# A two-layer decoder: where a projection group's last transpositions stand, and low parts in halves

## The chip, the cores and the metric

One core of a Trainium2 chip runs the whole program. The metric is the device time of one execution in microseconds (us), the median of several runs.

## The reference, cut to what matters

The program is a trunk of two layers over 2048 positions of width 1024, in float32. Layer A projects the normalised input to queries, keys, values, a forget logit per head and a gate, and attends causally with 16 heads. Layer B projects shared keys and values (4 heads), queries (16 heads) and a gate, and attends in a window of 128. Each attention ends with a gated output projection and a residual.

```python
u = rmsnorm(h, norm_a_g[i])
proj = u @ w_in_a[i]                       # q | k | v | forget logits | gate
q = rmsnorm(q.reshape(b, s, N_HEADS_A, HEAD_DIM), qnorm_a_g[i])
k = rmsnorm(k.reshape(b, s, N_HEADS_A, HEAD_DIM), knorm_a_g[i])
...
k_s, v_s = jnp.split(u_kv @ w_kv, [KV_WIDTH_B], axis=-1)
...
q, gate = jnp.split(u @ w_in_b[j], [WIDTH_B], axis=-1)
q = partial_rope(rmsnorm(q.reshape(b, s, N_Q_HEADS_B, HEAD_DIM), qnorm_b_g[j]), positions)
o = swa_sink_attention(q, k_shared, v_shared, sinks[j])
h = h + (o * jax.nn.silu(gate)) @ w_out_b[j]
```

## The kernel before, in words

Every float32 product is made of three products of rounded parts: a number is split into a high part (ACT rounds it, one copy) and a low part (DVE subtracts), and high x high, high x low and low x high are summed in PSUM.

`projections` runs twice, once for each layer. Its outer loop goes over column groups of the input weights: in layer A values, two key groups, three query groups (the first with the forget logits) and values again; in layer B the shared keys and values, two query groups and two gate groups. For a group, `weights` loads and splits its 8 weight tiles (ACT line 486, DVE line 487; `wh` and `wl` have nine buffers each, so the next group's tiles come in as the last block lets go of the old ones; the raw columns come through `wr`, two buffers of two tiles). Then, but for gate groups, comes a loop over the 16 blocks of 128 positions: 24 products of up to 512 columns (line 759) into one of three `b2` buffers of PSUM, and the block's norm (`qk_norm`: square on ACT, sums, reciprocal root and product on DVE; in layer B the rotary step too, partly on POOL, ending at DVE line 512), which leaves `qn` (two buffers).

`qn` must be transposed. That is `finish`: two to four transpositions on PE (line 349) into `pa` for even blocks and `pb` for odd ones, an eviction by ACT (line 524) and by DVE (line 525) into a staging tile `st`, and after each second block four stores on the SP queue (line 532). `finish` is not called at once but queued in the list `late`; with `QK_LAG = 1`, block t's job is taken out after the products of block t+2. So two jobs, those of blocks 14 and 15, are left when a group ends, and the loop `for job in late` calls them there, before the next group's weights and products.

`jobs` are side tasks of layer A at blocks 0, 3, 6 and 9 of each later group: splitting the gate's weight through three `st` tiles, or spilling the split input. A gate group (line 722) has 16 tiles of 24 products, into `pb` and `b2` (later `pa`) in turn, each followed by a gate evaluation on DVE, ACT and DVE. During the last gate group attention of layer B begins, through a hook.

`attention_b` is a generator of steps. In steps 4 to 11 `weight_split` makes the output weight's parts: a raw tile of two times 512 columns comes through `wr` (line 1420), ACT makes the high part (line 1433), DVE the low part (line 1434), each over 1024 columns. The output projection's products (line 1453) use them later. The exponentials of a step run on ACT at line 1323, the low parts of the transposed attention weights on DVE at line 1349.

The source order is not the order on an engine. A planner places the instructions at build time by its own estimate of durations: of those it takes to be ready, the one that stands first in the source. On the chip each engine then follows that order.

Of the kernel before, what the change touches and what calls it, by code (L numbers as in the profile page):

```python
# [18 lines left out]
ALU = mybir.AluOpType  # L19
# [41 lines left out]
QK_LAG = 1  # L61
# [37 lines left out]
def f_(ap):  # L99
    return ap.bitcast(F32)  # L100
# [51 lines left out]
class Trunk:  # L152
# [471 lines left out]
    def projections(self, normed, groups, row, later=None, pre=None, hook=None, first=None):  # L624

        nc, tc = self.nc, self.tc
        norm, factor, uh, ul, factors, _ = normed
        raw0 = None
        if pre is not None:
            raw0 = self.sb("big", [P, NDT, CH])

            def load_raw(dt):
                g0 = groups[0]
                nc.sync.dma_start(  # L640
                    out=raw0[:, dt : dt + 2, :],
                    in_=g0["w"][dt * P : (dt + 2) * P, g0["c0"] : g0["c0"] + CH].rearrange(
                        "(k p) c -> p k c", p=P
                    ),
                )

            norm(
                1,
                [partial(self.load_vectors, self.loads[:1])]
                + [partial(load_raw, dt) for dt in range(0, NDT, 2)],  # L650
            )
        else:
            norm(1)
        SW = 2 * P
        stages = {}
        z, forget = None, []

        def finish(q, qn, tb):
            t0 = (tb * P) % SW
            np_ = q["nh"] // 2  # L660
            if t0 == 0:
                stages[0] = tuple(self.sb("st", [P, np_, SW]) for _ in range(2))
            self.qk_transpose(qn, q["nh"], q["gain"], stages[0], t0, ("pa", "pb")[tb % 2])
            if t0 + P == SW:
                self.qk_store(
                    stages[0], q["dst"], q["p0"], np_, tb * P - t0, SW, q["hi_first"]
                )

        jobs = []
        if later is not None:  # L670
            wg, cg, gain, spill, wsplit = later

            def spill_u(ch, k, c0):
                t = (uh, ul)[k]
                c = slice(c0, c0 + NDT // 2)
                tc.keep_in_program_order(
                    nc.sync.dma_start(
                        out=spill[ch, k, c].rearrange("c p t -> p c t"), in_=f_(t[ch][:, c])
                    )
                )  # L680

            def split_w(dt):
                g = gain[:, dt : dt + 1]
                raw, hi, lo = (self.sb("st", [P, D]) for _ in range(3))
                nc.sync.dma_start(out=raw, in_=wg[dt * P : (dt + 1) * P, cg : cg + D])
                nc.scalar.activation(r_(hi), raw, AF.Copy, scale=g)
                nc.vector.scalar_tensor_tensor(r_(lo), raw, g, hi, ALU.mult, ALU.subtract)
                for k, t in enumerate((hi, lo)):
                    nc.sync.dma_start(
                        out=wsplit[:, :, dt // 2, k, dt % 2, :].rearrange("f p x -> p f x"),  # L690
                        in_=t.rearrange("p (f x) -> p f x", x=P),
                    )

            jobs = [partial(split_w, dt) for dt in range(NDT)]
            jobs += [
                partial(spill_u, ch, k, c0)
                for ch in range(NCH) for k in range(2) for c0 in (0, NDT // 2)
            ]

        for gi, grp in enumerate(groups):  # L700
            x2 = grp.get("extra")
            n = grp["n"] + (x2[1] if x2 else 0)
            if gi or first is None:
                W = self.weights(
                    grp["w"], grp["c0"], grp["n"], grp["gain"], x2, ahead=None if gi else raw0
                )
            else:
                W = first
            if gi == 0:
                norm(2)  # L710
            if "gate" in grp:
                f0, dst = grp["gate"]
                for ch in range(NCH):
                    rows = self.factor_rows(row, ch)
                    for ft in range(CH // P):
                        if hook is not None and gi == len(groups) - 1:
                            hook(ch * (CH // P) + ft)

                        ps = self.ps(("pb", "pa" if "fl" in self.banks else "b2")[ft % 2], [P, CH])
                        for dt in range(NDT):  # L720
                            for i, (k, u) in enumerate(((0, uh), (0, ul), (1, uh))):
                                nc.tensor.matmul(  # L722
                                    ps, W[k][dt][:, ft * P : (ft + 1) * P], u[ch][:, dt, :],
                                    start=(dt == 0 and i == 0),
                                    stop=(dt == NDT - 1 and i == 2),
                                )

                        sg = self.sb("sq", [P, CH])
                        nc.vector.tensor_tensor(sg, ps, rows, ALU.mult)
                        nc.scalar.activation(ps, sg, AF.Tanh)  # L730
                        nc.vector.scalar_tensor_tensor(sg, ps, 1.0, sg, ALU.add, ALU.mult)
                        fr = f0 + ft * P
                        nc.sync.dma_start(
                            out=dst[fr : fr + P, ch * CH : (ch + 1) * CH], in_=sg
                        )
                continue
            q, v = grp.get("qk"), grp.get("v")
            rope = self.rotary(q["rope"]) if q and "rope" in q else None
            late = []
            for tb in range(NTB):  # L740
                norm(tb + NORM_AHEAD)
                if gi == 1 and tb == ROW_AT:
                    self.rstd_row(factors, row)
                r0 = factors[:, tb : tb + 1]
                if gi == 0 and pre is not None and tb in pre:
                    pre[tb]()
                if tb in FORGET_AT and forget:
                    forget.pop(0)()
                if gi and tb in JOBS_AT and jobs:
                    jobs.pop(0)()  # L750
                us = slice(tb % 4 * P, (tb % 4 + 1) * P)
                ps = self.ps("b2", [P, CH])
                for dt in range(NDT):
                    if hook is not None and gi == len(groups) - 1:
                        hook(tb, dt)
                    if gi == 0:
                        factor(tb, dt)
                    for i, (u, k) in enumerate(((uh, 0), (uh, 1), (ul, 0))):
                        nc.tensor.matmul(  # L759
                            ps[:, :n], u[tb // 4][:, dt, us], W[k][dt],  # L760
                            start=(dt == 0 and i == 0), stop=(dt == NDT - 1 and i == 2),
                        )
                if len(late) > QK_LAG:
                    late.pop(0)()
                if q is not None:
                    c0 = q["c0"]
                    qn = self.qk_norm(
                        ps[:, c0 : c0 + q["nh"] * HD], q["nh"], tb, rope, r0
                    )
                    late.append(partial(finish, q, qn, tb))  # L770
                if grp.get("forget"):
                    if z is None:
                        z = self.sb("rot", [P, NTB, H])
                    nc.vector.scalar_tensor_tensor(
                        z[:, tb, :], ps[:, n - H : n], r0, self.bf, ALU.mult, ALU.add
                    )
                if v is not None:
                    self.v_tile(
                        ps[:, v["c0"] : v["c0"] + v["nh"] * HD], v["nh"],
                        v["dst"][v["h0"] : v["h0"] + v["nh"], tb * P : (tb + 1) * P, :].rearrange(  # L780
                            "h t e -> t h e"
                        ),
                        r0,
                    )
            for job in late:
                job()
            if grp.get("forget"):
                forget = self.forget(z)
        for job in forget:
            job()  # L790
# [467 lines left out]
    def attention_b(self, w_out, res, dst):  # L1258
# [168 lines left out]
        def weight_split(j):  # L1427
# [3 lines left out]
            h, lo = (W[half][t // 4][:, k, t % 4 : t % 4 + 2, :] for k in range(2))  # L1431
            raw = raws.pop(j)
            nc.scalar.copy(h, raw)
            nc.vector.tensor_tensor(lo, raw, f_(h), ALU.subtract)

        load(0)
        load_v(0)
# [185 lines left out]
```

## Time and profile before

| | us |
|---|---|
| median of 3 runs | 2460.58 |
| lowest, highest | 2459.92, 2462.29 |
| the profiled execution | 2461.66 |
| its span (first to last instruction) | 2459.7 |
| mean granted TensorE clock | 0.999 of full speed |

The profile is of one execution. A row of a timeline gives an instruction or several alike in a row; "idle before, and what ended it" is inferred from the semaphores. Products are pipelined, so their durations overlap: the step from start to start is the time that a product takes from PE. PE stands for TensorE's products and transpositions, PEld for its weight loads, DVE for VectorE, ACT for ScalarE, POOL for GpSimd, SP for the queue that issues the DMAs.

### The profile page before, as it was taken

The numbers are of one execution on the slowest core, as the hardware profiler recorded it, in microseconds if no ns is written. First come the engines' busy times: TensorE is split into PE (matmuls) and PEld (weight loads), VectorE is DVE, ScalarE is ACT, GpSimd is POOL, SyncE is SP. The second block draws the span as 40 slices with busy tenths as digits, with TensorE's granted clock in tenths as the row PEclk, the third lists the DMA queues.
The fourth block names the chain that finished last, engine by engine and source line by source line (L and its number), as shares of the span: only waits on it lengthen the run. The fifth ranks groups of instructions, "written<-read, shape, count | busy, mean of one in ns | idle before, by whom it ended". The sixth has DMA issues, their size and how long they took to land.

```text
span 2459.7 us, 36240 instructions
## 1 busy us (share of the span) xinstructions
PE 2424.1 (99%) x12016; PEld 2022.4 (82%) x12016; DVE 1727.4 (70%) x3826; ACT 1255.1 (51%) x2504; POOL 1001.9 (41%) x643
## 2 busy tenths in 40 slices
PE   8999999999999999999999999999999999999999
PEld 6788899988888887878877778888788888888887
DVE  7656567735888888888888866456766523777776
ACT  5433324323777777777777761135323312555554
POOL 0000000012877777777778862210011000377775
PEclk9999999999999999999999999999999999999999
DMA  6656545687554655465456649975434415555552
GB/s 181 207 165 193 156 145 168 192 261 223 168 155 128 210 141 150 143 198 164 133 168 182 169 137 306 290 253 153 139 90 120 137 64 165 174 176 178 180 180 73
DMA packets 351515, 419.24 MB, mean 170 GB/s; under 512 B 64928, under 2 KB 248256, under 8 KB 345152
## 3 DMA queue, kind: packets, MB, share of 16 engines
q1 hardware_dynamic: 351328, 416.92, 56.6%
q8 instruction: 95, 1.56, 0.3%
q14 instruction: 92, 0.75, 0.1%
HBM read 265.29 MB, written 151.40 MB: 169 GB/s over the span
## 4 chain that ended last, share of the span: by engine, by line
PE 46%; DVE 4%; DMA 2%; ACT 2%; POOL 2%; issue 2%; SPq 0%; DVEq 0%; ACTq 0%; POOLq 0%
PE b L759 9%; PE b L1240 5%; PE pa L1027 5%; PE pb L1453 4%; PE pb L722 3%; PE pb L1066 3%; PE b L722 3%; PE mx L936 2%; PE sc L985 2%; PE sc L984 2%; PE pa L1383 1%; PE b L1304 1%; PE pa L722 1%; PE pa L1240 1%; PE pb L1240 1%
## 5 line engine op out<-in xcount | busy, mean ns | idle before, releaser
L759 PE MATMUL b<-wh,big 128*128 128x512 f32 (+3 forms) x2560 | 770.1, 375 | 9.8 <-ACT wh L486 8.7
L1003 POOL TENSOR_TENSOR big<-st,big 128x1024 fp32r<-128x1024 f32 (+1 forms) x320 | 657.9, 2070 | 261.4 <-ACT big L1002 155.6
L759 PEld LDWEIGHTS b<-wh,big 128*128 128x128 f32 x2560 | 471.3, 188 | 81.2 <-ACT wh L486 10.5
L759 PE MATMUL b<-wl,big 128*128 128x512 f32 (+3 forms) x1280 | 474.2, 371 | 1.9 <-DVE wl L487 1.9
L1012 DVE TENSOR_TENSOR ac<-ac,st 128x512 f32<-128x512 f32 (+3 forms) x576 | 355.4, 617 | 55.6 <-ACT st L999 27.2
L999 ACT ACTIVATE st<-sc 128x512 f32<-128x512 f32 (+1 forms) x512 | 274.3, 585 | 161.8 <-PE sc L985 79.0
L1027 PE MATMUL pa<-big 128*128 128x512 f32 (+3 forms) x1280 | 326.1, 369 | 3.9 <-POOL big L1003 1.8
L1002 ACT CAST big<-st 128x1024 fp32r<-128x1024 f32 (+1 forms) x320 | 295.6, 924 | 7.8
L759 PEld LDWEIGHTS b<-wl,big 128*128 128x128 f32 x1280 | 241.4, 189 | 38.3 <-DVE wl L487 6.1
L1027 PEld LDWEIGHTS pa<-big 128*128 128x128 f32 x1280 | 222.0, 189 | 50.3 <-ACT sq L1035 17.0
L947 DVE CUSTOM_DVE_ANT_0 mx<-mx,rot 128x128 f32<-128x128 f32 (+3 forms) x240 | 210.7, 878 | 40.9 <-PE mx L936 34.8
L495 ACT ACTIVATE sq<-b,r 128x512 f32<-128x512 f32 (+2 forms) x128 | 77.8, 608 | 301.6 <-PE b L759 298.6
L984 PE MATMUL sc<-big 128*128 128x512 f32 (+3 forms) x640 | 230.1, 364 | 1.3 <-DVE st L542 1.1
L985 PE MATMUL sc<-big 67*128 67x512 f32 (+3 forms) x640 | 229.0, 367 | 0.0
L936 PE MATMUL mx<-big 66*128 66x128 f32 (+3 forms) x660 | 191.1, 363 | 3.6 <-DVE mt L947 3.1
L1066 PE MATMUL pb<-wh,wr 128*128 128x512 f32 x488 | 179.3, 398 | 2.8 <-DMA wr<-wg 2.2
L859 POOL MEMSET rot<- 128x1024 bf16 x1 | 1.0, 952 | 420.8 <-PE pb L349 420.8
L497 DVE TENSOR_REDUCE sm<-sq 128x8 f32<-128x512 f32 (+2 forms) x128 | 74.9, 585 | 138.6 <-ACT sq L495 138.4
L1352 POOL TENSOR_TENSOR big<-big,tri 128x1024 fp32r<-128x1024 f32 x60 | 143.8, 2397 | 67.1 <-DVE big L1349 62.2
L936 PEld LDWEIGHTS mx<-big 66*128 66x128 f32 x660 | 114.1, 190 | 40.9 <-DVE mt L947 11.9
L984 PEld LDWEIGHTS sc<-big 128*128 128x128 f32 x640 | 121.0, 189 | 23.1 <-DVE st L542 1.5
L985 PEld LDWEIGHTS sc<-big 67*128 67x128 f32 x640 | 121.2, 189 | 21.0
(281 smaller groups left out, 4124.8 us busy)
## 6 DMA issues: line engine op xcount, KB each, us to landing
wr<-wg SPq DMA_DIRECT2D x62, 512.0 KB
va<-st SPq DMA_DIRECT2D x32, 512.0 KB
ka<-st SPq DMA_DIRECT2D x64, 256.0 KB
ut<-big SPq DMA_DIRECT2D x16, 1024.0 KB
big<-ka SPq DMA_DIRECT2D x16, 1024.0 KB
big<-qa SPq DMA_DIRECT2D x16, 1024.0 KB
qb<-st SPq DMA_DIRECT2D x64, 256.0 KB
big<-qb SPq DMA_DIRECT2D x16, 1024.0 KB
```

Of the source, the lines that this page charges most:

```text
L722: nc.tensor.matmul(ps, W[k][dt][:, ft * P : (ft + 1) * P], u[ch][:, dt, :], start=(dt == 0 and i == 0), stop=(dt == NDT - 1 and i == 2),)
L759: nc.tensor.matmul(ps[:, :n], u[tb // 4][:, dt, us], W[k][dt], start=(dt == 0 and i == 0), stop=(dt == NDT - 1 and i == 2),)
L936: mm = nc.tensor.matmul(ps[:, b, :wb], qb[:66, i * P : (i + 1) * P], kb[:66, k0 + b * wb : k0 + (b + 1) * wb], start=True, stop=True,)
L947: nc.vector.tensor_tensor_reduce(out=lg, in0=lg, in1=mask, scale=1.0, scalar=NEG, op0=ALU.add, op1=ALU.max, accum_out=f_(o),)
L984: nc.tensor.matmul(o, ka[:, ks], qa[:, qs], start=not (last and n_), stop=False)
L985: nc.tensor.matmul(o, kb[:, ks], qb[:, qs], start=False, stop=not diag)
L999: nc.scalar.activation(pf[:, off : off + w], ps[:, :w], AF.Exp, scale=HD**-0.5)
L1002: nc.scalar.copy(ph[:, :tw], pf[:, :tw])
L1003: nc.gpsimd.tensor_tensor(pl[:, :tw], pf[:, :tw], f_(ph[:, :tw]), ALU.subtract)
L1012: nc.vector.tensor_tensor(a_, a_, pf[:, off : off + w], ALU.add)
L1027: nc.tensor.matmul(pv[:, q0 : q0 + w], v[:, k, :], src[:, off : off + w], start=(p == 0 and n_ == 0 and i == 0), stop=(last and n_ == 1 an ...
L1066: nc.tensor.matmul(ps, w[:, dt // 2 % 2, wk, dt % 2, :], us[dt][uk], start=(dt == 0 and i == 0), stop=(dt == NDT - 1 and i == 2),)
```

## The change

`late` is made once, ahead of the loop over the groups, and is no longer emptied at the end of each: the jobs of blocks 14 and 15 are taken out in the next group, after its products of blocks 0 and 1 (in a gate group after the products of its first two tiles; in the group of values, which queues none of its own, one after each block until the list is empty). Only after the last group whatever is left would be called. In `attention_b` the low part of the output weight is made by two DVE operations of 512 columns in place of one of 1024.

```diff
@@ projections
         stages = {}
+
+        late = []
         z, forget = None, []
...
                                     stop=(dt == NDT - 1 and i == 2),
                                 )
+                        if late:
+                            late.pop(0)()
 
                         sg = self.sb("sq", [P, CH])
...
             rope = self.rotary(q["rope"]) if q and "rope" in q else None
-            late = []
             for tb in range(NTB):
...
-                if len(late) > QK_LAG:
+                if late and (len(late) > QK_LAG or q is None):
                     late.pop(0)()
...
-            for job in late:
-                job()
+            if gi == len(groups) - 1:
+                for job in late:
+                    job()
@@ attention_b, weight_split
             nc.scalar.copy(h, raw)
-            nc.vector.tensor_tensor(lo, raw, f_(h), ALU.subtract)
+
+            for k in range(2):
+                nc.vector.tensor_tensor(lo[:, k], raw[:, k], f_(h)[:, k], ALU.subtract)
```

## Rows read from the trace of the kernel before

**Rows 1.** The page's first part: each engine's busy time in us, its share of the span, and its count of instructions.

```profile
PE 2424.1 (99%) x12016; PEld 2022.4 (82%) x12016; DVE 1727.4 (70%) x3826; ACT 1255.1 (51%) x2504; POOL 1001.9 (41%) x643
```

**Rows 2.** The list of who waited for whom, PE alone: PE's tile and line, what it waited for, us in total, times, the longest.

```profile
PE b L759 <- ACT wh L486: 8.7, 3, 8.2
...
PE pa L349 <- DVE qn L512: 1.0, 2, 0.5
...
PE pb L349 <- DVE qn L512: 0.6, 1, 0.6
```

**Rows 3.** PE's timeline at the end of layer B's first query group: start and duration in us, line, operation, out<-in, shapes, count, and in brackets the idle time before it with what ended it. `pa` takes the transpositions of even blocks, `pb` those of odd ones. The last row is from the chain that ended last: 24 products of 512 columns in a gate group.

```profile
1842.52 0.60 PE L349 MATMUL pa<-ident,qn 128*128 128x128 f32 x4
...
1842.87 0.48 PE L759 MATMUL b<-wh,big 128*128 128x512 f32 x1
...
1848.46 0.60 PE L349 MATMUL pb<-ident,qn 128*128 128x128 f32 x4
...
1849.57 0.63 PE L349 MATMUL pa<-ident,qn 128*128 128x128 f32 x4 [0.52 <-DVE qn L512]
...
1856.44 0.39 PE L759 MATMUL b<-wl,big 128*128 128x512 f32 x1
...
1856.88 0.63 PE L349 MATMUL pb<-ident,qn 128*128 128x128 f32 x4
...
1990.72 5.44 PE pb L722 x24
```

**Rows 4.** PE's timeline again: the first four rows where the key/value group hands over to the first query group, the last four where the second query group hands over to the first gate group.

```profile
1753.04 0.38 PE L349 MATMUL pb<-ident,qn 128*128 128x128 f32 x2
...
1753.43 0.41 PE L349 MATMUL pa<-ident,qn 128*128 128x128 f32 x2
...
1758.94 0.61 PE L759 MATMUL b<-wh,big 128*128 128x512 f32 x2
...
1760.20 0.41 PE L349 MATMUL pb<-ident,qn 128*128 128x128 f32 x2 [0.65 <-DVE qn L512]
...
1944.26 0.60 PE L349 MATMUL pb<-ident,qn 128*128 128x128 f32 x4
...
1945.38 0.63 PE L349 MATMUL pa<-ident,qn 128*128 128x128 f32 x4 [0.53 <-DVE qn L512]
...
1951.99 0.61 PE L722 MATMUL b<-big,wh 128*128 128x512 f32 x2
...
1952.70 0.63 PE L349 MATMUL pb<-ident,qn 128*128 128x128 f32 x4
```

**Rows 5.** The timeline in layer A: PE at the end of the first key group (two rows; the third is SP, the DMA queue, with the key stores of one pair of blocks), then PE at the first products of the fifth group and of the last.

```profile
199.43 0.60 PE L349 MATMUL pb<-ident,qn 128*128 128x128 f32 x4
...
199.86 0.60 PE L349 MATMUL pa<-ident,qn 128*128 128x128 f32 x4
...
200.98 3.18 SPq L532 DMA_DIRECT2D ka<-st  x4
...
374.43 0.44 PE L759 MATMUL b<-wh,big 128*128 128x384 f32 x1 [0.20 <-ACT wh L486]
...
503.59 0.50 PE L759 MATMUL b<-wl,big 128*128 128x512 f32 x1 [0.29 <-DVE wl L487]
```

**Rows 6.** The timeline of DVE at the end of layer B's first query group (three rows) and of ACT where layer A's last group begins (two rows).

```profile
1849.13 0.29 DVE L512 TENSOR_TENSOR qn<-ro,ro 128x128 f32<-128x128 f32 x1 [0.49 <-POOL ro L511]
...
1851.01 0.75 DVE L525 SCALAR_TENSOR_TENSOR st<-pa,g_qb,st 128x512 fp32r<-128x512 f32 x1 [0.15 <-ACT st L524]
...
1851.83 0.70 DVE L487 SCALAR_TENSOR_TENSOR wl<-wr,g_b,wh 128x512 fp32r<-128x512 f32 x1
...
498.86 0.72 ACT L486 ACTIVATE wh<-wr,g_a 128x512 fp32r<-128x512 f32 x1 [1.17 <-DMA wr<-in_w_in_a]
...
502.03 1.34 ACT L486 ACTIVATE wh<-wr,g_a 128x512 fp32r<-128x512 f32 x2 [1.11 <-DMA wr<-in_w_in_a]
```

**Rows 7.** Prices. First two rows of the view of line 1434 (count, then min/median/max in ns, first and last start; then who waited for it, us and times), then two groups of instructions with each shape apart (busy us, mean ns of one, idle before).

```profile
L1434 DVE TENSOR_TENSOR big<-wr,big x8: 1194/1216/1648, 2105.4 to 2156.0; 128x1024 fp32r<-128x1024 f32 x8
...
  PEld pb L1453: 0.5, 1
...
L1349 DVE TENSOR_TENSOR big<-fl,big 128x512 fp32r<-128x512 f32 x64 | 43.6, 682 | 0.8
...
L1198 DVE TENSOR_TENSOR wh<-wh 128x512 f32<-128x512 f32 x29 | 21.1, 729 | 0.9
```

**Rows 8.** The front of layer B's attention: the timeline of DVE, ACT and PE (five rows), then two stretches of 2 us: their length, busy time of PE (count), of PEld, DVE, ACT and POOL, the granted TensorE clock as a share of full speed, DMA share, GB/s.

```profile
2134.76 1.22 DVE L1434 TENSOR_TENSOR big<-wr,big 128x1024 fp32r<-128x1024 f32 x1 [0.17 <-ACT big L1433]
...
2141.55 1.05 ACT L1433 CAST big<-wr 128x1024 fp32r<-128x1024 f32 x1 [3.35 <-DMA wr<-in_w_out_b]
...
2144.19 1.21 PE L1304 MATMUL b<-big 128*128 128x256 f32 x8 [0.20 <-ACT st L1323]
...
2146.05 0.63 PE L349 MATMUL fl<-ident,st 128*128 128x128 f32 x4 [0.64 <-DVE big L1349]
...
2148.02 2.12 PE L1453 MATMUL pb<-big 128*128 128x512 f32 x6 [1.34 <-DVE sq L1459]
...
2148.00:2150.00 2.00, 1.98 (x7) 1.59 (x8) 1.97 (x5) 0.38 (x3) 2.00 (x3) 0.75 0.47 144
...
2150.00:2152.00 2.00, 2.00 (x6) 1.60 (x5) 0.43 (x2) 1.95 (x4) 0.76 (x2) 0.50 0.81 283
```

## The prediction, made before the changed kernel was run

> **What bounds the kernel now.** I read the page's line of busy times first. TensorE (PE) is busy 2424.1 of 2459.7 us; VectorE (DVE) 70%, ScalarE (ACT) 51% [rows 1]. So at most 2459.7 - 2424.1 = 35.6 us of visible idle can be won in the whole kernel, and the change touches a few places only. Next I read PE's list of waits: 8.7 us of it is for the high parts of weights, nearly all of that one wait of 8.2 us at the start, which the change doesn't reach; transpositions waiting for DVE to finish `qn` cost 1.0 + 0.6 us [rows 2]. Last I read PE's timeline around the eight places where a group with queries or keys hands over to the next group. The reader is to see there that a group's last transpositions do not stand where the source has them. In the steady state four transpositions take 1842.87 - 1842.52 = 0.35 us and nothing waits; at the end of the first query group of layer B block 13's follow the last product, block 14's come next and wait for DVE, and block 15's are already in among the next group's products [rows 3]. The order on an engine is thus a planner's, which puts first what it takes to be ready; the source sets the priority. A product of 512 columns steps at 5.44 / 24 = 0.23 us [rows 3].
>
> **Part 1, the transpositions.** Their count is unchanged (each still takes its 0.35 us, with an eviction on ACT and one on DVE and, every second block, four stores on SP); what can go is the idle time in front of them.
> - Layer B, query group to query group: block 14's start 1849.57 - 1848.46 = 1.11 us after block 13's, 0.35 of it work, so 0.76 idle. Block 15's start 0.44 us after the product ahead of them, 0.23 of it work: 0.21 idle. Together 0.97 [rows 3].
> - Key/value group to query group: block 14's two transpositions start 0.39 us after block 13's two (half of 0.35 = 0.18 is work): 0.21. Block 15's start 1.26 us after a pair of products (0.46 of work): 0.80. Together 1.01 [rows 4].
> - Query group to gate group: 1945.38 - 1944.26 - 0.35 = 0.77, and 1952.70 - 1951.99 - 0.46 = 0.25. Together 1.02 [rows 4].
> - Layer A has no rotary step, so `qn` is ready sooner: at the first such place 199.86 - 199.43 - 0.35 = 0.08. Five places make 0.4 [rows 5].
>
> Sum of what can go: 0.97 + 1.01 + 1.02 + 0.4 = 3.4 us. After the change the products of block 0 come first, and block 14's `qn` (DVE ends it at 1849.13 + 0.29 = 1849.4 [rows 6], 0.6 us after PE wanted it) is then needed up to 5.4 us later; that is the cover. What is late next is the weight. In the query-to-query case DVE evicts block 14's transpositions from 1851.01 and starts the next low part only at 1851.83 [rows 6]; with that eviction moved behind, the low part comes about 0.7 us sooner, while PE asks about 1 us sooner. A planner that knows this puts the transpositions, or the next block's products, into the hole, as it does with block 15's now; I take no loss here.
>
> In layer A three of the five places are limited by a weight's load: ACT stands idle 1.17 and 1.11 us for it [rows 6], and PE waits 0.20 us for a high part, 0.29 us for a low one [rows 5]. There the last transpositions are useful filler. If block 14's fall behind the wait instead of ahead of it, each place pays back 0.35 us. Bounds 0 and 3 x 0.35 = 1.05; I take the middle, 0.5.
>
> The stores: block 14/15's four stores hold SP for 3.18 us [rows 5] and SP is in order, so spills, prefetches and value stores behind them wait for an eviction that now comes one or two blocks later. I cost this at nothing: the stored blocks are read much later, in attention, and the next group's loads are early. The staging tiles (`st`, four buffers) are now asked for after the three of the weight job of block 0; an eviction that waits for them would hold ACT, and PE is covered by its three `b2` buffers, two blocks or 2 x 5.4 us. In the gate group block 15's transpositions use `pb`, which gate products 0 and 2 use too; the odd products, in `b2`, cover that. Each cover, were it gone, would cost one eviction, some 1.4 us (ACT, then DVE).
>
> Part 1: -3.4 + 0.5 = -2.9 us.
>
> **Part 2, the low parts in halves.** Eight DVE operations of 1024 columns (median 1.216 us) become sixteen of 512. The trace has no such low part of 512 columns; the nearest rows are a subtraction out of PSUM, 0.682, and a product in SBUF, 0.729 [rows 7]. So each pair costs between 2 x 0.682 - 1.216 = 0.15 and 2 x 0.729 - 1.216 = 0.24 us more; eight cost 1.2 to 1.9 us of DVE. During the gate products DVE has idle time and PE doesn't wait for it, so those cost nothing; only the last operations lie in attention's front, where PE waits. I take 0.3; bounds 1.9 (all on the path) and -0.5, as PE now waits 0.5 us once for a low part of which the first half could serve it sooner [rows 7].
>
> [...]
>
> Sum: -2.9 + 0.3 = -2.6 us. The profiled execution took 2461.66 us (span 2459.7 and about 2.0 around it), 1.1 above the median of the three runs; it would become 2459.1, and the median 2460.58 - 2.6 = **2458.0 us**.
>
> **The rivals.** A difference under 0.2% (4.9 us) is about what a measurement here cannot tell from no change.
> - *A, forecast:* the idle time ahead of the transpositions goes. 2458.0, own range 2456.5 (3.4 gone, 0.5 from halves) to 2460.5. Chance 0.46.
> - *B, the weights take the place:* PE comes 3.4 us sooner in all and finds the weights unsplit. For it: a low part takes DVE 0.70 us and its three products take PE 3 x 0.23 = 0.69 [rows 3, 6], and three places already wait for loads. Against it: in layer B no wait for a weight shows at these places. 2460.5. Chance 0.13.
> - *E, it doesn't do what it says:* the planner finds block 14's transpositions ready and leaves them behind block 13's. For it: the gate group's first product needs `pb`, still under eviction. Against it: block 0's products elsewhere need nothing late. 2460.3 (the halves alone). Chance 0.08.
> - *C, attention's front is put right too:* at 2142 to 2152 us ACT stands 3.35 us for one load of the output weight, which it took ahead of the exponentials; that load was issued when the low part before it, run from 2134.76, gave its buffer back. [...] Other sizes of operation give the planner another order, and it may put the exponentials ahead. For it: this is the one stall whose cause lies in lines the change edits. Against it: halves give the buffer back no sooner. 2458.0 - 3.7 = 2454.3. Chance 0.20.
> - *D, slower:* SP's queue. If the four stores come to stand ahead of a next group's weight load, it lands 3.18 us later [rows 5], and PE, already waiting for it in layer A, waits that much longer. One such place gives -2.6 + 3.2 = +0.6; it decides from the third on, as 2.6 + 4.9 = 7.5 us are needed; three give 2458.0 + 9.5 = 2467.5. Against it: in the changed source those stores come behind the next group's loads, and the planner follows the source among what is ready. Chance 0.13.
>
> **How the numbers follow.** A is likeliest, so 2458.0. The range reaches down past C's 2454.3 with the halves' better end and 3.4 in full (2452.5), and up to D with two places (2458.0 + 6.4 = 2464.4), so 2452.5 to 2464.5; about 0.1 lies above it (most of D) and little below. Faster by over 0.2%: C, 0.20, and 0.05 for A together with a part of C: 0.25. Slower: D, 0.13. Within: A's rest, B and E: 0.62.
>
> **What would show it.** Right: at the eight places block 14's transpositions stand behind at least nine products of the next group, and none of PE's waits is for `qn`; PE's idle time between 1753 and 1955 us shrinks by about 3 us. Wrong on the weights: PE's waits for `wh` and `wl` grow by what those for `qn` lose. C shows if ACT's wait of 3.35 us and the low clock are gone; D if ACT's waits for weight loads grow by 3 us each. The halves are right in price if they take 0.68 to 0.73 us. The forecast fails if the planner reorders attention's front, where one weight load in the wrong place weighs more than all eight hand-overs.

## The result: 0.24% slower, and where the trace shows it

The changed kernel took 2467.23 us, median of 9 runs (2463.29 to 2469.70), against 2460.94 for the kernel before (9 runs, 2458.31 to 2462.96): ratio 1.0024, 95% interval 1.0016 to 1.0033, so 3.9 to 8.1 us slower. The forecast was 2458.0 us, its range ended at 2464.5. The profiled execution took 2468.18 us.

The page's first lines of after. PE is busy 2426.8 us, 2.7 more than in [rows 1], in a span 6.8 longer: the idle time that was to shrink has grown, from 35.6 to 39.7 us.

```profile
span 2466.5 us, 36257 instructions
PE 2426.8 (98%) x12016; PEld 2025.1 (82%) x12016; DVE 1727.7 (70%) x3834; ACT 1254.9 (51%) x2504; POOL 1000.2 (41%) x643
```

PE's timeline of after where layer B's groups hand over, to set against [rows 3, 4] (line numbers after the change are up to 6 higher). First key/value to query, then query to query, then query to gate: block 13's transpositions, then block 14's.

```profile
1760.66 0.38 PE L349 MATMUL pb<-ident,qn 128*128 128x128 f32 x2
1766.40 0.38 PE L349 MATMUL pa<-ident,qn 128*128 128x128 f32 x2
...
1856.27 0.60 PE L349 MATMUL pb<-ident,qn 128*128 128x128 f32 x4
1862.49 0.60 PE L349 MATMUL pa<-ident,qn 128*128 128x128 f32 x4
...
1951.51 0.60 PE L349 MATMUL pb<-ident,qn 128*128 128x128 f32 x4
1952.62 0.63 PE L349 MATMUL pa<-ident,qn 128*128 128x128 f32 x4 [0.51 <-DVE qn L512]
```

At the first two places block 14's now come 5.7 and 6.2 us after block 13's, with block 0's products between them and no wait. At the gate group nothing has moved: 1.11 us apart, the same wait for `qn`. Layer A's five places show the change as well. What PE waited for there, from 110 to 600 us, is this list, for after:

```profile
PE b L762 <- ACT wh L486: 2.9, 5, 1.3
PE b L762 <- DVE wl L487: 1.0, 4, 0.3
```

and for before:

```profile
PE sc L984 <- DVE st L542: 1.1, 1, 1.1
PE b L759 <- DVE wl L487: 0.5, 2, 0.3
PE b L759 <- ACT wh L486: 0.5, 2, 0.3
```

Waits for split weights have grown from 1.0 to 3.9 us. (The 1.1 us before `sc` are attention A's; in after they stand at 600.23 us, just behind this window.) The halves of the low parts took this each (min/median/max in ns), in place of 1216:

```profile
L1440 DVE TENSOR_TENSOR big<-wr,big x16: 651/691/1081, 2112.7 to 2164.5; 128x512 fp32r<-128x512 f32 x16
```

To find where the time went I cut each trace at the same events. These are the four cuts of the first half, in before: the reduction of the norm (`qk_norm`) for block 15 of the first key group, the same for block 15 of the third query group, attention A's first score product, its last.

```profile
200.40 0.69 DVE L497 TENSOR_REDUCE sm<-sq 128x8 f32<-128x512 f32 x1 [1.12 <-ACT sq L495]
496.43 0.41 DVE L497 TENSOR_REDUCE sm<-sq 128x4 f32<-128x256 f32 x1
593.50 0.39 PE L984 MATMUL sc<-big 128*128 128x512 f32 x1
1466.10 0.28 PE L906 MATMUL sc<-fold,part 128*48 128x32 f32 x2
```

and in after:

```profile
201.03 0.69 DVE L497 TENSOR_REDUCE sm<-sq 128x8 f32<-128x512 f32 x1 [1.12 <-ACT sq L495]
500.09 0.41 DVE L497 TENSOR_REDUCE sm<-sq 128x4 f32<-128x256 f32 x1
598.50 0.39 PE L988 MATMUL sc<-big 128*128 128x512 f32 x1
1474.99 0.27 PE L910 MATMUL sc<-fold,part 128*48 128x32 f32 x2
```

Layer A's first four hand-overs lie between the first two cuts: 296.03 us before, 299.06 after, so +3.03. The last hand-over lies between the next two: 97.07 and 98.41, +1.34. Attention A: 872.60 and 876.49, +3.89, although its instructions stand in the same order on every engine. Two more cuts serve for layer B: from block 15 of the key/value group to the first gate product ("B's places", 192.03 us before), and from the ninth to the seventeenth row maximum of attention B ("B's front", 46.31). This table has them for every kernel profiled, as the difference from the first profile of before, in us; it is the working of all that follows.

```
                A: four   A: last   attention A   B's places   B's front
before again     -0.06     +0.48      +3.09         +0.12        -0.98
halves_only      +0.05     +0.34      +0.26         +0.39        -0.40
late_B           +0.28     +0.13      -0.36         -0.78        -1.56
late_B_gate      +0.03     -0.14      -1.23         -1.89        -2.71
shifted          -0.18     +0.08      -0.15         -0.05        +0.77
late_last        -0.23     +1.16      +1.41         +0.22        -2.52
late_first4      +2.80     +0.24      +1.09         +0.42        -2.73
late_A           +3.46     +0.73      +2.13         +0.27        -1.23
t_only           +3.17     +1.12      +2.81         -0.32        -2.72
t_only again     +3.09     +0.61      +1.55         -0.92        +2.90
after            +3.03     +1.34      +3.89         -0.39        -0.72
after again      +3.21     +0.80      +1.51         -0.64        -0.14
late_job         +2.13     +1.13      +1.34         -0.44        -3.67
middle           +0.02     +1.29      -0.70         +0.26        +1.83
before_noload    +0.18     -2.57      +0.06         -0.28        -0.27
t_noload         -1.22     -2.63      +2.33         -1.05        -1.53
```

### The profile page after: what moved, and what is told of

The parts are those of the page before. It is cut to its first block, busy times and chain, and to the rows that moved or that the text cites. A ratio compares the mean times of both kernels' runs of the same rounds, so it can differ in the third digit from the quotient of the medians.

```text
span 2466.5 us, 36257 instructions
## 1 busy us (share of the span) xinstructions
PE 2426.8 (98%) x12016; PEld 2025.1 (82%) x12016; DVE 1727.7 (70%) x3834; ACT 1254.9 (51%) x2504; POOL 1000.2 (41%) x643
## 4 chain that ended last, share of the span: by engine, by line
PE 46%; DVE 4%; DMA 2%; ACT 2%; POOL 2%; issue 2%; SPq 0%; DVEq 0%; ACTq 0%; POOLq 0%
PE b L762 10%; PE b L1244 5%; PE pa L1031 4%; PE pb L1459 4%; PE pb L1070 3%; PE pb L724 3%; PE b L724 3%; PE mx L940 2%; PE sc L989 2%; PE sc L988 2%; PE pa L1387 1%; PE b L1308 1%; PE pa L1244 1%; PE pb L1244 1%; PE pa L724 1%
```

## The experiments: which part, and which layer

Two theories stood after the comparison. W: in layer A TensorE now reaches the next group's weights before they are split. H: the halves, which give the planner another order for the whole of attention B, are the loss. Four kernels separate the parts; each was timed against before in the same series.

**t_only**: all of the transpositions' edit, the low part whole again.

```
-            for k in range(2):
-                nc.vector.tensor_tensor(lo[:, k], raw[:, k], f_(h)[:, k], ALU.subtract)
+            nc.vector.tensor_tensor(lo, raw, f_(h), ALU.subtract)
```

> The transpositions' part alone, the low parts of the output weight whole as before. Theory W (the next group's weights: in layer A PE now reaches them before they are split, +4.4 us there by the two traces; layer B's hand-overs give back 1.7): 2.5 to 7 us slower than before, the upper end if the 3.9 us that attention A lost with the same order of instructions belongs to it. Theory H (the halves, which reshuffle the whole of attention B, are the loss): within 1 us of before or faster.

Measured: 2465.37 against 2461.46 us, ratio 1.0018 (1.0009 to 1.0027), so 3.9 us slower, as W has it.

**halves_only**: the other part alone.

> The low parts in halves alone, the transpositions as before. Theory W: within 2 us of before. Theory H: 4 to 7 us slower. If the stall at attention B's front (3.7 us) goes with another order, 2 to 4 us faster.

Measured: 2461.68 against 2461.46, ratio 1.0002 (0.9993 to 1.0011).

**late_A** and **late_B**: the queue of late transpositions is carried over a hand-over in one layer only, and emptied at the group's end, as before, in the other.

```
-            if gi == len(groups) - 1:
-                for job in late:
-                    job()
+            if gi == len(groups) - 1 or later is None:        # late_A (late_B: is not None)
+                while late:
+                    late.pop(0)()
```

> The transpositions' part in layer A's five places only; layer B's three and the low parts as before. Theory W: slower by 4.4 us (the projections alone) to 8.3 (with attention A's 3.9). Theory H, or a loss that only layer B makes: within 1 us of before.

Measured: 2465.29, ratio 1.0019 (1.0010 to 1.0028): 3.8 us slower, a little less than W's 4.4 to 8.3.

> The transpositions' part in layer B's three places only; layer A's five and the low parts as before. Theory W: 1 to 2.5 us faster than before (1.7 in the traces; 3.0 was the term forecast for these three places). If layer B's places lose as well: slower.

Measured: 2459.87, ratio 0.9993 (0.9984 to 1.0002): 1.6 us faster by the medians, as W has it, but the interval reaches past no change.

H falls: the halves alone change nothing that can be measured, and their interval ends at 2.7 us, where H had 4 to 7. Layer A's five places alone cost as much as all eight. In the table the column of the first four places tells it best: the six profiles with the edit there (late_job, middle and those without loads aside) lie between +2.80 and +3.46, the six without it between -0.23 and +0.28.

## The experiments: why layer A loses

**late_job** asks TensorE for the same order as t_only, but lets the weight job of block 0 (the raw load of 512 KB of the gate's weight, its split and stores) be asked for after the late transpositions.

```
-                if gi and tb in JOBS_AT and jobs:
+                if gi and tb in JOBS_AT and jobs and not (tb == 0 and late):
                     jobs.pop(0)()
...
                 if late and (len(late) > QK_LAG or q is None):
                     late.pop(0)()
+                    if gi and tb == 0 and jobs:
+                        jobs.pop(0)()
```

> The transpositions' part in all places, but at a group's block 0 the weight job (the raw load of 512 KB of the gate's weight and its split) is asked for after the late transpositions, so that it stands behind the next group's weight loads again, as before. TensorE's order is that of the transpositions' part alone. Theory J (the job that came ahead of the weights at the first key group's end makes that place's loss): the loss there (1.0 us from block 15 of that group to block 2 of the next, by the q-norm's reductions) falls to 0.5 or less, the four other places of layer A lose as before (3.1 to 3.4 us). Theory F (only the moved filler counts): 1.0 us there as well.

Measured (one run): 2459.96 us against 2461.48, which says nothing of the edit, as attention B's front alone was 3.67 us shorter here. At the first key group's end 0.2 us were gained where t_only lost 1.0, so theory J holds for that place; the first four places together lost 2.13 in place of 3.1. The timeline of SP, ACT and PE at that place in after shows what the job had done:

```profile
193.83 0.35 SPq L687 DMA_DIRECT2D st<-in_w_in_a  x1
197.19 1.84 SPq L440 DMA_DIRECT2D wr<-in_w_in_a  x2
198.42 1.15 ACT L688 ACTIVATE st<-st,g_a 128x1024 fp32r<-128x1024 f32 x1 [0.84 <-DMA st<-in_w_in_a]
204.66 1.33 ACT L486 ACTIVATE wh<-wr,g_a 128x512 fp32r<-128x512 f32 x2 [1.77 <-DMA wr<-in_w_in_a]
205.43 0.49 PE L762 MATMUL b<-wh,big 128*128 128x512 f32 x1 [0.65 <-ACT wh L486]
```

and in before:

```profile
196.57 1.85 SPq L440 DMA_DIRECT2D wr<-in_w_in_a  x2
202.12 1.98 ACT L486 ACTIVATE wh<-wr,g_a 128x512 fp32r<-128x512 f32 x3
205.59 0.35 SPq L685 DMA_DIRECT2D st<-in_w_in_a  x1
```

The job's three `st` tiles are now asked for ahead of block 14's staging tiles, so its load goes out at 193.8 in place of 205.6 us, ahead of the next group's last two weight loads. Those land later, ACT waits 1.77 us for them, and PE 0.65 us for the high part and 0.29 us for the low one. In late_job the load stands at 205.17 us again and ACT's wait is 0.17:

```profile
202.54 1.34 ACT L486 ACTIVATE wh<-wr,g_a 128x512 fp32r<-128x512 f32 x2 [0.17 <-DMA wr<-in_w_in_a]
205.17 0.35 SPq L687 DMA_DIRECT2D st<-in_w_in_a  x1
```

The other places remain. For them theory F: block 14's transpositions were filler ahead of a weight that lands at its own time. There are two `wr` buffers, so the last two of a group's four weight loads go out when the first two are split (at 196.57 us in before, above), and that is when the group before gives its `wh` tiles back, in its last block. Two kernels leave out these late loads.

**before_noload** and **t_noload**: of each weight of layer A's groups after the first, tiles 4 to 7 are split out of the rows loaded for tiles 0 to 3.

```
-            elif dt % 2 == 0:
+            elif gain is self.g_a and dt >= 4:
+                raws = kept[dt // 2 - 2]
+            elif dt % 2 == 0:
                 raws = self.sb(tag, [P, 2, CH])[:, :, :tw]
...
+            if dt % 2 == 0:
+                kept.append(raws)
             raw = raws[:, dt % 2, :]
```

> The kernel before, but of each of layer A's weights the tiles 4 to 7 are split out of the raw rows of tiles 0 to 3 (with the gains of 4 to 7): half of the loads of these weights are left out, and none is late. The output is not the reference's. Theory F (the last transpositions filled time in which TensorE waits for the last weights' loads): TensorE's waits for weights at layer A's hand-overs are gone (0.6 us less or more), and layer A's projections end 0.5 to 2 us earlier than before.

> The transpositions' part alone, with the same half of layer A's weight loads left out; the output is not the reference's. Compared with the kernel before with the same loads left out. Theory F (filler ahead of late loads): no loss in layer A without late loads, -0.5 to +1.0 us instead of +4.2 to +4.3. A theory by which the loss comes from elsewhere (order on DVE and ACT, the stores, the jobs): +3 to +4.5 us as with the loads.

PE's list of waits from 110 to 600 us is one line in before_noload and the same line in t_noload:

```profile
PE sc L992 <- DVE st L546: 1.1, 1, 1.1
```

No weight is waited for in either. Then the edit gains time: t_noload's first four places are 1.40 us shorter than before_noload's (-1.22 - 0.18), its last one 0.06. With the loads the same edit lost 3.1 + 0.8. (One run each: 2460.30 and 2456.73 us. From the first cut to attention A before_noload is 2.4 us shorter than before, somewhat more than the 0.5 to 2 expected.) So the loss needs the late loads: the new order on DVE, the stores and the jobs cost nothing where no load is late, and the job of the first place cost its 1.2 us by way of the loads that it held up. The pair also takes away half of the load traffic; the next kernel keeps it all.

**middle** keeps the loads and puts the filler back where it was wanted: block 14's transpositions are asked for in the middle of block 0's products, and the job after them.

```
+                    if tb == 0 and dt == 4 and len(late) > 1:
+                        late.pop(0)()
...
-                if late and (len(late) > QK_LAG or q is None):
+                if late and (len(late) > (QK_LAG if tb else 0) or q is None):
```

(and, as in late_job, the weight job of block 0 behind the transpositions)

> The late transpositions go among the next group's products, but into the middle of block 0's (block 14's after the products of four of the eight weight tiles, just ahead of where layer A waits for the fifth; block 15's behind block 0's), and the weight job of block 0 after them; low parts whole. Theory F: layer A loses 0 to 1 us instead of 4.2, layer B keeps what it won (0.5 to 1.5 us): 0.5 to 2 us faster than before. If any move of them costs layer A's time: 3 to 5 us slower, as the transpositions' part alone.

Measured: 2463.41 against 2461.48 us, ratio 1.0006 (0.9997 to 1.0015). The first four places cost nothing (+0.02), as F has it: with the transpositions back ahead of the late weights, and the job behind them, the loss is gone. The last place still lost 1.29, and F doesn't explain that. There block 14's transpositions stand ahead of the first late weight and block 15's just behind it, in the kernel before as in middle, and the last two weights are split at the same time. ACT's split and PE, in the second profile of the kernel before (taken further below):

```profile
500.52 0.38 PE L349 MATMUL pb<-ident,qn 128*128 128x128 f32 x2
503.21 1.34 ACT L486 ACTIVATE wh<-wr,g_a 128x512 fp32r<-128x512 f32 x2 [1.74 <-DMA wr<-in_w_in_a]
503.99 0.50 PE L762 MATMUL b<-wh,big 128*128 128x512 f32 x1 [0.55 <-ACT wh L486]
```

and in middle:

```profile
500.63 0.38 PE L349 MATMUL pb<-ident,qn 128*128 128x128 f32 x2
503.19 1.33 ACT L486 ACTIVATE wh<-wr,g_a 128x512 fp32r<-128x512 f32 x2 [1.98 <-DMA wr<-in_w_in_a]
503.96 0.50 PE L764 MATMUL b<-wh,big 128*128 128x512 f32 x1 [1.33 <-ACT wh L486]
```

Between block 15's last product and that wait for the seventh weight PE ran 25 products before the change and 21 in middle. (late_B and halves_only, which leave layer A as it was, have 25 too, t_only 22.) Block 0 has only 3 x 6 = 18 for the first six weights, so the others, 7 and 3, are of the next block. The four that are missing are 4 x 0.23 = 0.9 us, and the wait is 0.8 us longer. So there is a second kind of filler, products of block 1 run in among block 0's, and with the edit the planner uses less of it; at the last place that is the loss beyond the 0.48 us that the same place scattered by in before. Why the planner uses less was not looked into.

Layer B won nothing in middle (+0.26): block 14's transpositions no longer wait, but block 15's, asked for right behind block 0's products, now do, at the first two of B's places (and the gate group's wait is as it was):

```profile
1761.34 0.41 PE L349 MATMUL pb<-ident,qn 128*128 128x128 f32 x2 [1.02 <-DVE qn L512]
...
1857.60 0.63 PE L349 MATMUL pb<-ident,qn 128*128 128x128 f32 x4 [0.54 <-DVE qn L512]
```

So the gain expected of this kernel didn't come.

## The experiments: attention A, and what a profile can tell of it

Up to here attention A was 1.3 to 3.9 us longer in each profile with the edit in layer A but middle's, where it was 0.7 shorter. **late_last** and **late_first4** carry the queue at layer A's last place only, or at the first four only; **shifted** is the kernel before with 18 products more in the middle of the first key group.

```
+            if gi == len(groups) - 1 or later is None or gi != 5:   # late_last; late_first4: gi == 5
...
+                    if later is not None and gi == 1 and tb == 8 and dt == 0:
+                        for _ in range(18):
+                            nc.tensor.matmul(
+                                ps[:, :n], uh[tb // 4][:, 0, us], W[0][0], start=True, stop=True
+                            )
```

> The transpositions' part at one place only, layer A's last (third query group to second value group, ahead of attention A); all else as before. Attention A lost 1.3 to 3.9 us in each kernel with the part in layer A and -0.7 to +0.3 in each without, with the same order of instructions there. Theory S (what this last place leaves behind, its loads and stores in another order just ahead of attention A, makes attention A longer): this place 0.7 to 1.3 us and attention A +1.3 us or more. Theory P (anything that comes later in time meets attention A's loads in another phase): attention A within 0.5 us, as only 1 us is shifted.

> The transpositions' part at layer A's first four places only, not at the last one ahead of attention A; all else as before. Theory F: 3.0 to 3.4 us lost up to block 15 of the third query group and about 0.3 at the last place. Theory S: attention A within 0.5 us of before. Theory P: attention A +1.3 us or more.

> The kernel before with 18 products more of 512 columns ahead of block 8 of the first key group (their result is overwritten), which is 18 x 0.23 = 4.1 us of TensorE's time; the order of all else on every engine is that of before. Theory P (a mere shift in time makes attention A longer): attention A +1.3 us or more, the whole 5.4 us or more slower than before. Theory S: attention A within 0.5 us, the whole 4.1 us slower.

Measured, one run each beside 2458.26 us for before: 2461.11, 2461.45 and 2464.84. Attention A was +1.41, +1.09 and -0.15. Neither theory fits: both parts of layer A's edit show it, so not the last place alone, and a shift of 4 us shows none. (As a whole, shifted took 6.6 us longer than the median of before, where P had 5.4 or more and S 4.1; one run can't tell these apart, as before's own 15 runs lie between 2456.73 and 2462.05.) The places themselves add up: 2.80 for the first four, 1.16 for the last. Then the same programs were profiled again.

> The kernel before once more (same program). If attention A's difference belongs to the program: attention A, from its first score product to its last, within 0.7 us of the first profile's 872.6 us. If it belongs to the execution: off by 1 to 3 us.

> The changed kernel once more (same program). Program: attention A 3 to 4.5 us longer than in the profile of before, layer A's projections 4.2 to 4.5 longer. Execution: attention A anywhere from 0 to 4 us longer, layer A's projections as said.

> The transpositions' part alone once more (same program). Program: attention A 2.3 to 3.3 us longer than in the profile of before. Execution: anywhere from 0 to 4. Attention B's front (from the eighth to the sixteenth row maximum, 2.7 us shorter than before at first): the same question.

These are single runs: the kernel before took 2465.46 and 2463.72 us here, the changed one 2464.00, t_only 2468.08. So in this series the whole doesn't show the loss, which is within the scatter of single runs; layer A's places show it in both profiles. Attention A of the kernel before took 875.69 us the second time, 3.09 more than the first, nearly as much as the difference in question. After's second was +1.51 (first +3.89), t_only's +1.55 (first +2.81). So a single profile's figure for attention A belongs to the execution as much as to the program. On average the nine profiles with the edit in layer A (middle, with -0.70, aside) show +2.0 there and the seven without it, the first of before among them, +0.2: all nine lie at +1.09 or more, of the seven only the second profile of before. Whether that is more than scatter stays open. B's front scatters more: 43.59 us in t_only's first profile, 49.21 in its second, with the same instructions. First the one, then the other, by the load of the output weight that ACT waits for there and by two stretches of 4 us (columns as in [rows 8]):

```profile
2146.28 1.05 ACT L1437 CAST big<-wr 128x1024 fp32r<-128x1024 f32 x1 [1.82 <-DMA wr<-in_w_out_b]
...
2150.00:2154.00 4.00, 2.90 (x19) 2.42 (x18) 3.94 (x10) 2.47 (x10) 3.28 (x2) 1.00 0.50 175
2154.00:2158.00 4.00, 3.65 (x20) 2.97 (x18) 2.38 (x6) 3.19 (x11) 2.46 (x4) 1.00 0.67 222
```

```profile
2144.68 1.05 ACT L1437 CAST big<-wr 128x1024 fp32r<-128x1024 f32 x1 [3.05 <-DMA wr<-in_w_out_b]
...
2150.00:2154.00 4.00, 2.57 (x9) 1.98 (x10) 3.90 (x10) 1.81 (x9) 3.98 (x3) 0.61 0.45 149
2154.00:2158.00 4.00, 4.00 (x12) 3.10 (x11) 2.40 (x5) 3.89 (x13) 2.46 (x3) 0.53 0.55 190
```

In the second profile ACT waited 1.2 us longer for the load. PE then stood idle for 1.55 and 1.34 us with four transpositions between, and the granted clock was 0.61 and 0.53 of full speed in the two stretches. In the first PE's waits of 1.10 and 1.19 us lie 6 us apart and the clock was 1.00 up to 2162 us:

```profile
2150.09 0.63 PE L349 MATMUL fl<-ident,st 128*128 128x128 f32 x4 [1.55 <-DVE big L1353]
...
2152.06 2.93 PE L1459 MATMUL pb<-big 128*128 128x512 f32 x6 [1.34 <-DVE sq L1465]
```

A lower clock doesn't follow such idle time every time: the second profile of the kernel before has 1.27 and 1.35 us at the same two instructions, also with four transpositions between, and its six products behind them took 1.66 us, where those above took 2.93 (in the first profile of t_only, at a clock of 1.00, they took 1.66 as well):

```profile
2151.02 0.63 PE L349 MATMUL fl<-ident,st 128*128 128x128 f32 x4 [1.27 <-DVE big L1353]
...
2152.99 1.66 PE L1459 MATMUL pb<-big 128*128 128x512 f32 x6 [1.35 <-DVE sq L1465]
```

That the longer wait for the load set off the 5.6 us is inferred from the order of events; no run moved that load alone.

**late_B_gate** looks for a version that beats both: late_B, and the first gate group begins with buffer `b2` in place of `pb`.

```
-                        ps = self.ps(("pb", "pa" if "fl" in self.banks else "b2")[ft % 2], [P, CH])
+                        ps = self.ps(("pb", "pa" if "fl" in self.banks else "b2")[(ft + (gi == 3)) % 2], [P, CH])
```

> The transpositions' part in layer B's three places only, and the first gate group's products in the other order of buffers (product 0 in b2, product 1 in pb), so that its first product needs no buffer under eviction: block 14's transpositions can go behind it. Low parts whole. Theory: the wait for qn ahead of the gate group goes (0.8 to 1.0 us more than with layer B's part alone), 1.5 to 3.5 us faster than before. If gate products that start in b2 run into other waits: no faster than layer B's part alone (0.9993), or slower.

Measured: 2457.16 against 2458.26 us, ratio 0.9997 (0.9988 to 1.0006), so better than the changed kernel (1.0024). But the 1.5 to 3.5 us expected didn't come: the interval includes no change. Block 14's transpositions now do move at the gate group:

```profile
1941.83 0.60 PE L349 MATMUL pb<-ident,qn 128*128 128x128 f32 x4
1942.18 0.71 PE L724 MATMUL b<-big,wh 128*128 128x512 f32 x2
...
1947.76 0.60 PE L349 MATMUL pa<-ident,qn 128*128 128x128 f32 x4
```

and the stretch from the second query group's block 15 (its reduction) to the first gate product is 1.16 us shorter than before; in late_B it is 0.02 shorter.

## Why the prediction was wrong, point by point

- *Layer A, the step that failed.* "Five places make 0.4" and "each place pays back 0.35 ... I take the middle, 0.5" gave +0.1 us net. Measured: 3.0 to 3.2 for the first four places and 0.6 to 1.3 for the last (t_only and after, twice each), of which kernels without the edit show 0 and about 0.2. So +3.9. The mechanism was named, filler that falls behind a late weight, but mis-sized. I counted three places, at half a set of transpositions each; the rows showed PE waiting at two only. In fact the second to fourth lost 0.5 to 0.9 us each, more than the 0.35 of a set. The first has no late weight in before and was given one by the job. And I left out a filler: in before the planner had run products of block 1 in among block 0's where a weight was late; in after it let block 14's transpositions stand in for them, or nothing. PE's waits for weights grew by 2.9 of the 4.4 us that the five places lost in after's first profile. At the last place middle shows what the missing products of block 1 cost by themselves, 0.8 us, as much as t_only and after lost there on average; at the others their part was not measured by itself.
- *The weight job.* The text saw that block 0's job now asks for `st` ahead of the staging tiles and feared for an eviction. What it moved was a transfer: 512 KB ahead of two weight loads, about 1.2 us at one place.
- *Layer B, forecast -3.0.* Key/value to query: -0.9 to -1.0 in t_only and after, as forecast (1.01). Query to query: -0.3 to -0.8, of 0.97. Query to gate: 0 of 1.02; rival E was right for this one place, since the first gate product needs `pb`, and late_B_gate shows it by taking that need away. Inside the first query group another wait grew: the row of factors is turned over in `pa`, its eviction (L414) stands on DVE behind a block's norm, and the transpositions behind it wait, 0.6 to 0.95 us in the four profiles of t_only and after; in before it is 0 in the first profile and 0.33 in the second. In after:

```profile
1772.33 0.27 PE L349 MATMUL pa<-ident,r 128*16 128x128 f32 x1
...
1778.71 0.28 DVE L414 TENSOR_SCALAR ro<-pa 16x128 f32<-16x128 f32 x1
...
1779.05 0.65 PE L349 MATMUL pa<-ident,qn 128*128 128x128 f32 x4 [0.95 <-DVE ro L414]
```

  Net: -0.3 to -0.9 against +0.23 on average without the edit, so -0.8 of the 3.0.
- *The halves.* Right in price: 2 x 691 - 1216 = 166 ns a pair (0.15 to 0.24 us forecast). The 0.3 us taken for them can't be told from nothing (halves_only, 1.0002).
- *The rivals.* B's mechanism decided, but in layer A, and with loss, not as a gain that fails to come. D's direction was right, its cause not: no wait for a weight grew by 3 us, and no store did it, though at one place a load ahead of the weights did. C: in after ACT still waits 3.43 us for the load and the clock is still low (0.63 and 0.51 from 2154 to 2158 us), so the front was not put right; but it scatters by 5.6 us in one program. No run shows the 3.7 us taken for it as a term of its own; what was measured is that scatter, and PE's waits and the clock in [rows 8]. The closing sentence looked for a failure at attention's front; the forecast failed at the hand-overs.
- *The sum by what repeats:* +3.1 + 0.8 - 0.8 = +3.1 us. That is inside t_only's interval (2.2 to 6.6 us) and 0.8 below after's (3.9 to 8.1). What more after lost, if it did, stays open; attention A's +2.0 against +0.2 would cover it, but that can't be told from scatter.

## What to carry to other kernels

Work that "waits for nothing" ahead of a late transfer is filler. Moving it behind the transfer cost more than its length here (0.5 to 0.9 us a place for 0.35 us of transpositions); at the one place where the two could be told apart it was the next block's products, kept out by the new order, that were missing. Before moving it, ask for every place what TensorE will do until the last weight has landed. A moved step also moves its requests for buffers, and whatever was queued for the same buffers goes first (here a load of 512 KB, at 193.8 in place of 205.6 us); look on the DMA queue for what overtakes. And profile the unchanged program twice before reading a stage's difference of a few us from two traces (attention A of the kernel before differed by 3.09 us between its two).

## What the runs showed that I had not expected

With the same program, attention A took 872.60 and 875.69 us (before) and attention B's front 43.59 and 49.21 (t_only), while layer A's first four hand-overs repeated to 0.2 us or better (296.03 and 295.97 in before) and its last to 0.5. Attention A waits for loads of its own (PE 2.2 us in the first profile of before, 3.2 in that of after); that this makes its scatter was not shown. And TensorE's clock can't be read off its idle time in such rows alone: behind two waits of 1.27 and 1.35 us close together six products took 1.66 us in one execution, as at a clock of 1.00, and behind 0.64 and 1.34 the clock was 0.75 and then 0.50 [rows 8] in another of the same kernel.
